# Padding 48-row products to 128 rows, and alternating the two heads of a pair, in the state-space branch of a hybrid decoder block

## The chip, the cores and the metric

The kernel runs on one core of one Trainium2 chip. The metric is the device time of one execution in microseconds. A core has a matrix engine (TensorE: PE in the profile, and PEld for its weight loads), a vector engine (DVE), a scalar engine (ACT), a general engine (POOL) and a queue engine (SP) that here only issues transfers. About 0.2% (some 2 us) is what a measurement of this kernel can tell from no change.

## The reference

One layer of a gated block over 512 tokens of width 1024, in float32: a normalisation, one wide input projection, three token mixers (a state-space scan, a top-k attention, a pooling mixer), each up-projected and gated, one output projection, a feed-forward part and a last normalisation. The change lies in the state-space scan. It has 16 heads of width 64 in 2 groups, and works on 4 chunks of 128 tokens:

```python
a_cs = jnp.cumsum(a, axis=2)
seg = a_cs[:, :, :, None] - a_cs[:, :, None, :]
lmat = jnp.exp(jnp.where(causal, seg, -jnp.inf))
cb = jnp.einsum('bclgn,bcsgn->bclsg', Cc, Bc)
y_diag = jnp.einsum('bclsg,bclsgj,bcsgjp->bclgjp', cb, lmat, x)
...
y_off = jnp.einsum('bclgn,bcgjpn,bclgj->bclgjp', Cc, prev, jnp.exp(a_cs))
return (y_diag + y_off).reshape(b, T, g, j, p).astype(out_dtype)
```

So each head needs its running sum `a_cs` spread over a 128x128 square per chunk (for `lmat`), and again over its 64 output rows (for `exp(a_cs)`).

## The kernel before

Large products are feature-major: weights are split into a high and a low part (`wh` by ACT, `wl` by DVE), and each group of 128 output features takes 8 steps of three 128x512 matmuls (`product`, L244 to L250) into a PSUM tile `mm`, `up` or `f`. These fill the matrix engine from start to end. After every step `tick()` lets a stream of small work put its next few matmuls between the big ones: the attention heads, then the scan. The matrix engine runs its instructions in the order in which the program writes them (a count of estimated costs in `_Clock` decides when a stream may step); the other engines' order is set by a scheduler. All small products take PSUM tiles named by their use.

The scan works in pairs of heads, `ssd_pair(f)` for f from 0 to 7, two pairs in progress at a time (L800 to L845). For each of the two heads:

- `seg` (L812): one matmul of the head's running sum, kept in `acsT`, against a column of `sel`, so that every one of 128 output rows holds that sum for all 512 tokens. `acsT` holds 48 rows: the sums of 16 heads in a rounded part, a second copy, and a rest part; `sel` picks a head's rows. The matmul contracts over these 48 rows.
- `L` (L813 to L818): DVE takes the minimum with `acs`, ACT makes four exponentials of 128x128, DVE multiplies by `cbt`.

Then for the pair: `ebc` (L822) spreads the sums over the pair's 128 output rows (again 48 rows contracted, 384 columns), ACT makes `E` of it. `yd` (L825 to L830) is the in-chunk product: for each head and chunk one float32 matmul with 64 output rows, head 0 to rows 0 to 63 of the tile and head 1 to rows 64 to 127. In the trace a float32 matmul is two passes, so the 8 matmuls are 16 records. `yo` (L834) is the part that comes from the state, 128 rows and 128 columns, and DVE and POOL put the parts together. `acsT` and `sel` are written long before, in the prologue and in `dt_prep` (L525 to L529).

A matmul row of the profile such as `seg<-acsT,sel 48*128 48x512` contracts over 48 rows, has 128 output rows and streams 512 columns; `128*64` has 64 output rows.

Of the kernel before, what the change touches and what calls it, by code (L numbers as in the profile page):

```python
# [8 lines left out]
F32 = mybir.dt.float32  # L9
R32 = mybir.dt.float32r  # L10
AF = mybir.ActivationFunctionType
OP = mybir.AluOpType

P = 128
T = 512
D = 1024
NT = T // P
# [43 lines left out]


class _Engine:
    """Forwards to an engine and keeps an estimate of the work queued on it."""

    def __init__(self, name, eng, clock):
        self.name, self.eng, self.clock = name, eng, clock
# [28 lines left out]
def kernel(  # L96
# [25 lines left out]
    PE, ACT = _Engine("PE", nc.tensor, clk), _Engine("ACT", nc.scalar, clk)  # L122
    DVE, POOL = _Engine("DVE", nc.vector, clk), _Engine("POOL", nc.gpsimd, clk)
# [9 lines left out]
    streams = []  # L133

    class Stream:
        """Chains of work that fill in between the steps of the big products, up to `width` of them at once."""

        def __init__(self, gens, width, urgent=False):
            self.gens, self.width, self.live, self.urgent = list(gens), width, [], urgent
# [48 lines left out]
    def nm(s):  # L188
        uid[0] += 1
        return f"{s}_{uid[0]}"  # L190

    def const(shape, name, dtype=F32):
        return cpool.tile(shape, dtype, name=name, tag=name)

    def slot(tag, name, dtype=F32, shape=(P, T)):
        return spool.tile(list(shape), dtype, name=nm(name), tag=tag, bufs=SLOTS[tag])

    def small(shape, name, bufs=2, dtype=F32):
        return tiny.tile(list(shape), dtype, name=nm(name), tag=name, bufs=bufs)
# [10 lines left out]
    def tsl(t):  # L210
        return slice(t * P, (t + 1) * P)
# [39 lines left out]

    halves = (slice(0, T // 2), slice(T // 2, T))

# [1 line left out]
    win = w_in[0]  # L255
    xf = x[0]
    ones = const([P, P], "ones")
# [23 lines left out]
    ident = const([P, P], "ident")  # L281
# [86 lines left out]
            evac(ps)  # L368
        job(lambda: split_w(src, (P, KD, P)), body)

# [1 line left out]
    def stack(src, tag, name):  # L372
        outs = []
        for a in range(2):
# [21 lines left out]
    first = [split_w(r, (P, KD, P), e) for r, e in ((raw0[:, :, tsl(0)], POOL), (raw0[:, :, tsl(1)], POOL), (raw1[:, :, tsl(0)], DVE))]  # L396
# [16 lines left out]
    expA = const([P, 16], "expA")  # L413
    SP.dma_start(expA, row_bcast(a_log, 16))

    sel = const([48, 16], "sel", R32)
    DVE.tensor_tensor(sel, ident[0:48, 0:16], ident[0:48, 32:48], op=OP.add)
    DVE.reciprocal(ratio, ratio)
    for g in range(4):
        DVE.tensor_scalar(ratio[:, g, :], ratio[:, g, :], float(2 << g), None, OP.mult)  # L420
# [63 lines left out]
    def dt_prep():  # L484
        n = NT * 16
        dv = dt.rearrange("p c h -> p (c h)")
        tc.keep_in_program_order(ACT.activation(expA, expA, AF.Exp))
        ab = small([P, n], "sp0", 1)
        DVE.scalar_tensor_tensor(ab, dv, -1.0, dv, OP.mult, OP.max)
        e = small([P, n], "sp1", 1)  # L490
        ACT.activation(e, ab, AF.Exp, scale=-1.0)
        den = ab
        DVE.tensor_scalar(den, e, 2.0, None, OP.add)
        DVE.reciprocal(den, den)
        s = e
        DVE.tensor_tensor(s, e, den, op=OP.mult)
        z = den
        DVE.tensor_tensor(z, s, s, op=OP.mult)
        q = small([P, n], "sp2", 1)
        DVE.tensor_scalar(q, z, 1.0 / 15.0, None, OP.mult)  # L500
        for c in (13.0, 11.0, 9.0, 7.0, 5.0, 3.0):
            DVE.scalar_tensor_tensor(q, q, 1.0 / c, z, OP.add, OP.mult)
        DVE.scalar_tensor_tensor(q, q, 1.0, s, OP.add, OP.mult)
        DVE.tensor_scalar(dv, dv, 0.0, None, OP.max)
        DVE.scalar_tensor_tensor(dv, q, 2.0, dv, OP.mult, OP.add)
        a = small([P, NT, 16], "sa", 1)
        DVE.scalar_tensor_tensor(a, dt, -1.0, expA[:, None, :].to_broadcast([P, NT, 16]), OP.mult, OP.mult)
        a3 = small([P, NT, 3, 16], "a3", 1)
        DVE.tensor_copy(a3, a[:, :, None, :].to_broadcast([P, NT, 3, 16]))
        av = a.rearrange("p c h -> p (c h)")  # L510
        yield
        ps = paux("acs")
        PE.matmul(ps[:, 0:n], lhsT=triu, rhs=av, start=True, stop=True)
        acv = acs.rearrange("p c h -> p (c h)")
        DVE.tensor_copy(acv, ps[:, 0:n])
        DVE.tensor_scalar(nacs.rearrange("p c h -> p (c h)"), acv, -1.0, None, OP.mult)
        yield
        ps = paux("alast")
        PE.matmul(ps[:, 0:n], lhsT=ones, rhs=av, start=True, stop=True)
        ACT.activation(dch.rearrange("p c h -> p (c h)"), ps[:, 0:n], AF.Exp)  # L520
        dec = small([P, n], "sp1", 1)
        DVE.tensor_tensor(dec, ps[:, 0:n], acv, op=OP.subtract)
        ACT.activation(decay.rearrange("p c h -> p (c h)"), dec, AF.Exp)
        yield
        ps = paux("acsT")  # L525
        for c in range(NT):
            PE.matmul(ps[0:48, tsl(c)], lhsT=a3[:, c].rearrange("p r h -> p (r h)"), rhs=triu, start=True, stop=True)
        ACT.copy(acsT, ps[0:48, :])
        DVE.tensor_tensor(acsT[32:48, :], ps[32:48, :], acsT[32:48, :], op=OP.subtract)  # L529
        yield  # L530

# [1 line left out]
    nacs = const([P, NT, 16], "nacs")  # L533
    dch = const([P, NT, 16], "dch")
    decay = const([P, NT, 16], "decay")
    acsT = const([48, T], "acsT", R32)

    bias = [None] + [slot("A", "bias") for _ in range(3)]
    picked = {0}
    Stream([kd_tokens()] + [scores(b, bias[b]) for b in range(1, NT)] + [dt_prep()]  # L540
           + [topk(b, bias[b]) for b in range(1, NT)], 1)

# [1 line left out]
    pw = slot("m", "poolw", shape=(P, 4, P))  # L544
    AQ.dma_start(pw, pool_w[0].rearrange("g c d -> c g d"))
    pwh = slot("m", "poolwh", R32, (P, 4, P))
# [43 lines left out]
        for s in range(2):  # L590
            proj_job(raw[:, :, tsl(s)], pool_evac(2 * j + s))

# [1 line left out]
    def k_evac(ps):  # L594
        kT.extend(double(ps, g, "T2", "kT") for g in range(2))

# [128 lines left out]
        for st in mixes:  # L725
            need(st)

# [1 line left out]
    xbc = [None] * 12  # L729

    def conv_evac(f):
# [12 lines left out]
            xbc[f] = hv  # L744
        return evac

# [1 line left out]
    zs = [None] * KD  # L748
    ssq = []
    ctx_g = [dict(xdt=[], hst=[None]) for _ in range(2)]  # L750
# [7 lines left out]
    def ssd_group(g):  # L758
        G = ctx_g[g]
        BT, CT = xbc[8 + g], xbc[10 + g]  # L760
        G["selp"] = slot("T2", "selp", R32, (48, 4, P))
        DVE.tensor_copy(G["selp"].rearrange("a b (c d) -> a (b c) d", d=64),
                        sel[:, 8 * g:8 * g + 8][:, :, None].to_broadcast([48, 8, 64]))
        ps = paux("btr")
        for c in range(NT):
            PE.transpose(ps[:, tsl(c)], BT[:, tsl(c)], ident)
        btok = slot("A", "btok")
        ACT.copy(btok, ps)
        G["btok"] = btok
        ps = paux("cbt")  # L770
        for c in range(NT):
            PE.matmul(ps[:, tsl(c)], lhsT=BT[:, tsl(c)], rhs=CT[:, tsl(c)], start=True, stop=True)
        cbt = slot("A", "cbt")
        DVE.tensor_tensor(cbt.rearrange("p (c t) -> p c t", c=NT), ps.rearrange("p (c t) -> p c t", c=NT),
                          triu[:, None, :].to_broadcast([P, NT, P]), op=OP.mult)
        G["cbt"] = cbt
        for c in range(NT):
            yield
            ps = paux("xtr")
            for i in range(4):  # L780
                PE.transpose(ps[:, tsl(i)], xbc[4 * g + i][:, tsl(c)], ident)
            xd = slot("A", "xdt")
            DVE.tensor_tensor(h8(xd), h8(ps), b8(dt, c, g), op=OP.mult)
            G["xdt"].append(xd)
            if c == NT - 1:
                break
            xdd = slot("T1", "xdd")
            POOL.tensor_tensor(h8(xdd), h8(xd), b8(decay, c, g), op=OP.mult)
            yield
            ps = paux("state")  # L790
            PE.matmul(ps, lhsT=btok[:, tsl(c)], rhs=xdd, start=True, stop=True)
            hn = slot("T2", "hst")
            if c == 0:
                ACT.copy(hn, ps)
            else:
                POOL.tensor_tensor(h8(hn), h8(G["hst"][c]), b8(dch, c, g), op=OP.mult)
                DVE.tensor_tensor(hn, hn, ps, op=OP.add)
            G["hst"].append(hn)

    def ssd_pair(f):  # L800
        g, pr = divmod(f, 4)
        G = ctx_g[g]
# [6 lines left out]
        for hh in range(2):  # L809
            j = 2 * f + hh  # L810
            ps = paux("seg")
            PE.matmul(ps, lhsT=sel[:, j:j + 1].to_broadcast([48, P]), rhs=acsT, start=True, stop=True)  # L812
            l = slot("T1", "L")  # L813
            DVE.tensor_tensor(l.rearrange("p (c t) -> p c t", c=NT), ps.rearrange("p (c t) -> p c t", c=NT),
                              acs[:, :, j:j + 1].to_broadcast([P, NT, P]), op=OP.min)
            for c in range(NT):
                ACT.activation(l[:, tsl(c)], l[:, tsl(c)], AF.Exp, bias=nacs[:, c, j:j + 1])
            DVE.tensor_tensor(l, l, G["cbt"], op=OP.mult)  # L818
            L.append(l)
            yield  # L820
        ps = paux("ebc")
# [1 line left out]
        E = slot("T1", "E")  # L823
        ACT.activation(E[:, P:], ps[:, P:], AF.Exp)
        yd = paux("yd")  # L825
        for hh in range(2):
            jl = 2 * pr + hh
            for c in range(NT):
                PE.matmul(yd[hh * 64:hh * 64 + 64, tsl(c)], lhsT=G["xdt"][c][:, jl * 64:jl * 64 + 64], rhs=L[hh][:, tsl(c)],
                          start=True, stop=True)  # L830
        DVE.scalar_tensor_tensor(xT, xT, c_dskip(f), yd, OP.mult, OP.add)
# [111 lines left out]
    gate_merge(0, w_up_ssd, 8, lambda k: ysh[k], lambda k: ysl[k], ssd_ready)  # L943
    flush()

# [1 line left out]
    def start_now(gen):  # L947
        st = Stream([gen], 1, urgent=True)
        at = clk.pe
# [122 lines left out]
    for j in range(NH // 2):  # L1072
# [12 lines left out]
        for s in range(2):  # L1085
            i = 2 * j + s
            pab = []
            for key, r in ((("a", i), ra), (("b", i), rb)):
# [4 lines left out]
                ps = pmm("f")  # L1093
# [18 lines left out]
    of = out[0]  # L1112
# [34 lines left out]
```

## Time and profile before

| | |
|---|---|
| median of 3 runs | 942.32 us (942.07 to 942.43) |
| the profiled execution, its span | 942.4 us |
| matrix engine busy | 920.5 us |
| DVE, ACT, POOL busy | 491.0, 359.8, 94.6 us |
| transfers | 85.42 MB, 91 GB/s |
| scan pairs on the matrix engine | first `seg` at 321.8 us, last `yd` at 417.8 us |

The page gives the span of the profiled execution and no other time of it; it lies 0.1 us from the median. "Busy" of the matrix engine is to be read with care: a record lasts longer than the step to the next one, since matmuls are pipelined. The time that a matmul takes from the engine is the distance from its start to the start of the next. A row of the timeline gives start, length, engine, line and operands, and in brackets the idle time before it and what ended it. All instructions that go through the kernel's engine wrapper carry line L90, so the operands tell them apart.

### The profile page before, as it was taken

The numbers are of one execution on the slowest core, as the hardware profiler recorded it, in microseconds if no ns is written. First come the engines' busy times: TensorE is split into PE (matmuls) and PEld (weight loads), VectorE is DVE, ScalarE is ACT, GpSimd is POOL, SyncE is SP. The second block draws the span as 40 slices with busy tenths as digits, with TensorE's granted clock in tenths as the row PEclk, the third lists the DMA queues.
The fourth block names the chain that finished last, engine by engine and source line by source line (L and its number), as shares of the span: only waits on it lengthen the run. The fifth ranks groups of instructions, "written<-read, shape, count | busy, mean of one in ns | idle before, by whom it ended". The sixth has DMA issues, their size and how long they took to land.

```text
span 942.4 us, 10998 instructions
## 1 busy us (share of the span) xinstructions
PE 920.5 (98%) x4401; PEld 755.8 (80%) x4401; DVE 491.0 (52%) x792; ACT 359.8 (38%) x618; POOL 94.6 (10%) x94
## 2 busy tenths in 40 slices
PE   6999899999999999999999999999999999999997
PEld 4887678888888777777888889888888888888885
DVE  6487999955654565668333455333333333322226
ACT  5446433355563344435323247223223223212114
POOL 2061000001111132232000013000000000000001
PEclk9999999999999999999999999999999999999999
DMA  7132112222212211134323241222222233233212
GB/s 236 46 112 84 52 45 90 87 92 89 89 47 63 94 45 57 46 100 148 121 90 125 98 135 45 90 90 90 90 90 89 90 104 119 90 97 122 94 45 89
DMA packets 70964, 85.42 MB, mean 91 GB/s; under 512 B 4025, under 2 KB 61953, under 8 KB 70914
## 3 DMA queue, kind: packets, MB, share of 16 engines
q1 hardware_dynamic: 69234, 82.38, 27.0%
q10 hardware_dynamic: 1680, 2.36, 0.7%
q8 instruction: 34, 0.56, 0.2%
q14 instruction: 16, 0.13, 0.0%
HBM read 82.63 MB, written 2.10 MB: 90 GB/s over the span
## 4 chain that ended last, share of the span: by engine, by line
PE 88%; DVE 8%; ACT 1%; issue 1%; POOL 1%; DMA 1%; SPq 0%; ACTq 0%; POOLq 0%; DVEq 0%
PE mm L90 28%; PE f L90 26%; PE acc L90 17%; PE up L90 8%; DVE work L90 2%; DVE wl L90 2%; PE yatt L90 1%; PE yd L90 1%; DVE top L90 1%; PE ptr L90 1%; PE logit L90 1%; PE yo L90 1%; PE seg L90 1%; POOL win L90 1%; DVE qT L90 1%
## 5 line engine op out<-in xcount | busy, mean ns | idle before, releaser
L90 DVE TENSOR_TENSOR wl<-raw,wh 128x1024 fp32r<-128x1024 f32 (+1 forms) x150 | 184.5, 1230 | 228.3 <-ACT wh L90 223.1
L90 ACT CAST wh<-raw 128x1024 fp32r<-128x1024 f32 (+1 forms) x152 | 152.7, 1005 | 383.1 <-PE f L90 155.7
L90 PE MATMUL mm<-xnh,wh 128*128 128x512 f32 (+1 forms) x480 | 196.3, 409 | 0.2 <-ACT xnh L90 0.2
L90 PE MATMUL mm<-xnl,wh 128*128 128x512 f32 (+1 forms) x480 | 184.6, 384 | 1.2 <-DVE xnl L90 1.2
L90 PE MATMUL mm<-xnh,wl 128*128 128x512 f32 (+1 forms) x480 | 184.8, 385 | 0.0
L90 PE MATMUL f<-hnh,wh 128*128 128x512 f32 x328 | 127.6, 389 | 0.0
L90 PE MATMUL f<-hnl,wh 128*128 128x512 f32 x328 | 127.6, 389 | 0.0
L90 PE MATMUL f<-hnh,wl 128*128 128x512 f32 x328 | 127.6, 389 | 0.0
L90 PEld LDWEIGHTS mm<-xnh,wh 128*128 128x128 f32 x480 | 92.5, 193 | 18.3 <-issue 4.8
L90 PEld LDWEIGHTS mm<-xnh,wl 128*128 128x128 f32 x480 | 91.8, 191 | 18.3 <-DVE wl L90 0.3
L90 PEld LDWEIGHTS mm<-xnl,wh 128*128 128x128 f32 x480 | 92.3, 192 | 15.8 <-DVE xnl L90 1.7
L90 PEld LDWEIGHTS f<-hnl,wh 128*128 128x128 f32 x328 | 61.6, 188 | 12.9
L90 PEld LDWEIGHTS f<-hnh,wh 128*128 128x128 f32 x328 | 61.6, 188 | 12.8
L90 PEld LDWEIGHTS f<-hnh,wl 128*128 128x128 f32 x328 | 61.6, 188 | 12.6
L90 DVE TENSOR_TENSOR silu<-silu,f 128x512 f32<-128x512 f32 x22 | 15.1, 688 | 78.5 <-PE f L90 78.5
L90 PE MATMUL acc<-wh,hidh 128*128 128x512 f32 x144 | 56.0, 389 | 0.0
L90 PE MATMUL acc<-wl,hidh 128*128 128x512 f32 x144 | 56.0, 389 | 0.0
L90 PE MATMUL acc<-wh,hidl 128*128 128x512 f32 x144 | 44.8, 389 | 0.0
L90 POOL TENSOR_TENSOR rows<-xr,fnrow 128x512 f32<-128x512 f32 x3 | 3.9, 1290 | 353.0 <-issue 347.4
L90 POOL TENSOR_TENSOR xbc<-xbc,tap 128x509 f32<-128x509 f32 x12 | 14.0, 1164 | 195.5 <-DVE xbc L90 167.9
L90 PEld LDWEIGHTS acc<-wh,hidh 128*128 128x128 f32 x144 | 27.0, 188 | 5.6
L90 PEld LDWEIGHTS acc<-wh,hidl 128*128 128x128 f32 x144 | 27.0, 188 | 5.6
(248 smaller groups left out, 1330.6 us busy)
## 6 DMA issues: line engine op xcount, KB each, us to landing
raw<-in_w_in_dram SPq DMA_DIRECT2D x26, 1024.0 KB, 5.0
raw<-in_w_ffn_in_dram SPq DMA_DIRECT2D x22, 1024.0 KB, 4.9
raw<-in_w_ffn_out_dram SPq DMA_DIRECT2D x11, 1024.0 KB, 5.0
raw<-in_w_up_ssd_dram SPq DMA_DIRECT2D x4, 1024.0 KB, 4.9
raw<-in_w_out_dram SPq DMA_DIRECT2D x4, 1024.0 KB, 5.0
xb<-in_x_dram SPq DMA_DIRECT2D x4, 512.0 KB, 4.1
raw<-in_w_in_dram SPq DMA_DIRECT2D x4, 512.0 KB, 6.0
raw<-in_w_up_pool_dram SPq DMA_DIRECT2D x2, 1024.0 KB, 5.2
```

The source lines that it names most:

```text
L90: return fn(*args, **kw)
```

## The change

`sel`, `acsT` and `selp` get 128 rows in place of 48. `sel` and `acsT` are set to zero once on POOL, and the code then writes their first 48 rows as before. The matmuls `seg` and `ebc` so contract over 128 rows, 80 of which are zero. In `yd` the loops over heads and chunks change places: the heads alternate. Some comments and docstrings are gone as well.

```diff
-    sel = const([48, 16], "sel", R32)
-    DVE.tensor_tensor(sel, ident[0:48, 0:16], ident[0:48, 32:48], op=OP.add)
+    sel = const([P, 16], "sel", R32)
+    POOL.memset(sel.bitcast(F32), 0.0)
+    DVE.tensor_tensor(sel[0:48, :], ident[0:48, 0:16], ident[0:48, 32:48], op=OP.add)
...
-        ACT.copy(acsT, ps[0:48, :])
+        ACT.copy(acsT[0:48, :], ps[0:48, :])
...
-    acsT = const([48, T], "acsT", R32)
+    acsT = const([P, T], "acsT", R32)
+    POOL.memset(acsT.bitcast(F32), 0.0)
...
-        G["selp"] = slot("T2", "selp", R32, (48, 4, P))
+        G["selp"] = slot("T2", "selp", R32, (P, 4, P))
...
-            PE.matmul(ps, lhsT=sel[:, j:j + 1].to_broadcast([48, P]), rhs=acsT, start=True, stop=True)
+            PE.matmul(ps, lhsT=sel[:, j:j + 1].to_broadcast([P, P]), rhs=acsT, start=True, stop=True)
...
-        for hh in range(2):
-            jl = 2 * pr + hh
-            for c in range(NT):
+        for c in range(NT):
+            for hh in range(2):
+                jl = 2 * pr + hh
                 PE.matmul(yd[hh * 64:hh * 64 + 64, tsl(c)], lhsT=G["xdt"][c][:, jl * 64:jl * 64 + 64], rhs=L[hh][:, tsl(c)],
```

On the matrix engine the first pair stands so before. The number behind a name is that of the buffer: `L_2828` is head 0, `L_2888` head 1, and the four `xdt` are the four chunks.

```order
L90 MATMUL ebc_2946<-acsT,selp_2631 128x384 [waits DVE_49]
L90 MATMUL yd_2950<-L_2828,xdt_2664 64x128 [waits DVE_49,Activation_49]
L90 MATMUL yd_2950<-L_2828,xdt_2706 64x128 [waits Activation_49]
L90 MATMUL yd_2950<-L_2828,xdt_2753 64x128 [waits Activation_49]
L90 MATMUL yd_2950<-L_2828,xdt_2805 64x128 [waits Activation_49]
L90 MATMUL yd_2950<-L_2888,xdt_2664 64x128 [waits DVE_49]
L90 MATMUL yd_2950<-L_2888,xdt_2706 64x128 [waits Activation_49]
L90 MATMUL yd_2950<-L_2888,xdt_2753 64x128 [waits Activation_49]
L90 MATMUL yd_2950<-L_2888,xdt_2805 64x128 [waits Activation_49]
L90 MATMUL yo_2960<-xbc_1945,hst_2693 128x128 [waits Activation_49]
```

And so now, at the same place of the matrix engine's order (two buffers more come before it, so all numbers are higher by 2: `L_2830` is head 0, `L_2890` head 1).

```order
L90 MATMUL ebc_2948<-acsT,selp_2633 128x384 [waits DVE_49]
L90 MATMUL yd_2952<-L_2830,xdt_2666 64x128 [waits DVE_49,Activation_49]
L90 MATMUL yd_2952<-L_2890,xdt_2666 64x128 [waits DVE_49]
L90 MATMUL yd_2952<-L_2830,xdt_2708 64x128
L90 MATMUL yd_2952<-L_2890,xdt_2708 64x128 [waits Activation_49]
L90 MATMUL yd_2952<-L_2830,xdt_2755 64x128
L90 MATMUL yd_2952<-L_2890,xdt_2755 64x128 [waits Activation_49]
L90 MATMUL yd_2952<-L_2830,xdt_2807 64x128
L90 MATMUL yd_2952<-L_2890,xdt_2807 64x128 [waits Activation_49]
L90 MATMUL yo_2962<-xbc_1947,hst_2695 128x128 [waits Activation_49]
```

The wait for head 1's `L` (a DVE wait) has moved from the fifth `yd` to the second. No other matmul of the program changes its place.

On POOL, in the prologue, the two fills stand between the constants and the first weight split.

```order
L90 AFFINE_SELECT negc<-negc 128x128 [waits Pool_49]
L90 AFFINE_SELECT triu<-triu 128x128 [waits Pool_49]
L90 MEMSET sel 128x16
L90 MEMSET acsT 128x512
L90 TENSOR_TENSOR wl_167<-raw_82,wh_166 128x1024 [waits DMAHW4_49,Activation_49]
```

Before, the first `wl` follows the second `AFFINE_SELECT` at once. The one other move is on ACT, in the middle of the scan, where a weight copy `wh` and a gate evacuation `gth` stood so before.

```order
L90 ACTIVATE sq_631_3202<-xbc_426_2218 128x512 [waits DVE_49,PE_49]
L90 ACTIVATE gth_634_3226<-mm_619_3137 128x512 [waits PE_49]
L90 CAST wh_638_3247<-raw_616_3131 128x512
L90 ACTIVATE L_633_3219<-L_633_3219,nacs_424 128x128 [waits DVE_49]
L90 ACTIVATE L_633_3219<-L_633_3219,nacs_424 128x128 x3
```

Now the copy comes first, and both come before the same exponentials.

```order
L90 ACTIVATE sq_631_3204<-xbc_426_2220 128x512 [waits DVE_49,PE_49]
L90 CAST wh_638_3249<-raw_616_3133 128x512 [waits PE_49]
L90 ACTIVATE gth_634_3228<-mm_619_3139 128x512 [waits PE_49]
L90 ACTIVATE L_633_3221<-L_633_3221,nacs_425 128x128 [waits DVE_49]
L90 ACTIVATE L_633_3221<-L_633_3221,nacs_425 128x128 x3
```

The orders of DVE and SP are the same as before.

## Rows read from the trace of the kernel before

**Rows 1.** The page: busy time of the matrix engine with its share and count, and the chain that ended last by engine.

```profile
PE 920.5 (98%) x4401; PEld 755.8 (80%) x4401; DVE 491.0 (52%) x792; ACT 359.8 (38%) x618; POOL 94.6 (10%) x94
PE 88%; DVE 8%; ACT 1%; issue 1%; POOL 1%; DMA 1%; SPq 0%; ACTq 0%; POOLq 0%; DVEq 0%
```

**Rows 2.** Busy time by stage, the scan and all that follows it up to the tail: length, then busy time and count of PE, PEld, DVE, ACT, POOL, then the granted clock of the matrix engine, DMA share and GB/s.

```profile
290.00:424.00 134.00, 133.62 (x661) 100.32 (x660) 79.69 (x104) 53.86 (x117) 34.36 (x29) 1.00 0.22 71
424.00:930.00 506.00, 505.28 (x2320) 421.41 (x2319) 191.67 (x219) 158.08 (x216) 20.10 (x14) 1.00 0.29 97
```

**Rows 3.** Whom the matrix engine waited for between 280 and 520 us: total, times, longest.

```profile
PE rstd L90 <- ACT rt L90: 0.7, 1, 0.7
PE yd L90 <- DVE L L90: 0.4, 1, 0.4
```

**Rows 4.** Timeline of the matrix engine around a `seg` matmul (the tenth of sixteen).

```profile
376.78 0.39 PE L90 MATMUL mm<-xnh,wl 128*128 128x512 f32 x1
377.10 0.50 PE L90 MATMUL seg<-acsT,sel 48*128 48x512 f32 x1
377.52 0.50 PE L90 MATMUL mm<-xnh,wh 128*128 128x512 f32 x1
377.86 0.40 PE L90 MATMUL mm<-xnl,wh 128*128 128x512 f32 x1
```

**Rows 5.** Timeline of the matrix engine around `mix`, another small product put between the big ones, of the pooling branch: same type and columns as `seg`, but 128 rows.

```profile
54.23 0.39 PE L90 MATMUL mm<-xnh,wl 128*128 128x512 f32 x1
54.46 0.39 PE L90 MATMUL mix<-uh,poolwh 128*128 128x512 f32 x1
54.68 0.39 PE L90 MATMUL mix<-ul,poolwh 128*128 128x512 f32 x1
54.91 0.39 PE L90 MATMUL mix<-uh,poolwl 128*128 128x512 f32 x1
```

**Rows 6.** All `seg` matmuls: count, duration in ns (least, median, most), first and last start.

```profile
L90 PE MATMUL seg<-acsT,sel x16: 491/497/499, 321.8 to 411.7; 48*128 48x512 f32 x16
```

**Rows 7.** Timeline of the matrix engine at the end of the seventh pair.

```profile
402.54 0.39 PE L90 MATMUL mm<-xnh,wl 128*128 128x512 f32 x1
402.86 0.44 PE L90 MATMUL ebc<-acsT,selp 48*128 48x384 f32 x1
403.23 1.58 PE L90 MATMUL yd<-L,xdt 128*64 128x128 f32 x16
404.74 0.94 PE L90 MATMUL yo<-xbc,hst 128*128 128x128 f32 x6
```

**Rows 8.** Timeline of the matrix engine at `acsT`, the one other place where a product with few output rows (48) follows a full one.

```profile
99.30 0.39 PE L90 MATMUL mm<-xnh,wl 128*128 128x512 f32 x1
99.62 1.07 PE L90 MATMUL acsT<-triu,a 128*48 128x128 f32 x8
```

**Rows 9.** Timeline of the matrix engine at the end of the eighth pair, where head 1's `L` came late.

```profile
415.48 1.09 PE L90 MATMUL yd<-L,xdt 128*64 128x128 f32 x8
416.94 1.09 PE L90 MATMUL yd<-L,xdt 128*64 128x128 f32 x8 [0.38 <-DVE L L90]
417.96 0.94 PE L90 MATMUL yo<-xbc,hst 128*128 128x128 f32 x6
```

**Rows 10.** The `yd` instructions alone, in stretches of 0.22 us: length, then busy time and count of records of PE, PEld and DVE, the clock, DMA. The first row is of the fourth pair, where head 0 runs alone; the others are of the second pair, at its start and in its middle.

```profile
366.83:367.05 0.22, 0.22 (x4) 0.22 (x3) 0.00 (x0) 1.00 0.00 0
...
342.43:342.65 0.22, 0.22 (x4) 0.22 (x3) 0.00 (x0) 1.00 0.00 0
342.87:343.09 0.22, 0.22 (x7) 0.22 (x5) 0.00 (x0) 1.00 0.00 0
```

**Rows 11.** Timeline around the third and fourth pair: DVE's last step of `L` for the third, the matrix engine at the third and the fourth, and DVE's last step of `L` for the fourth.

```profile
361.84 0.69 DVE L90 TENSOR_TENSOR L<-L,cbt 128x512 f32<-128x512 f32 x1
...
362.75 1.58 PE L90 MATMUL yd<-L,xdt 128*64 128x128 f32 x16
...
365.72 0.60 PE L90 MATMUL xtr<-ident,xbc 128*128 128x128 f32 x4
...
366.62 2.18 PE L90 MATMUL yd<-L,xdt 128*64 128x128 f32 x16
...
366.36 0.69 DVE L90 TENSOR_TENSOR xdt<-xtr,dt 128x512 f32<-128x512 f32 x1 [0.50 <-PE xtr L90]
366.97 0.68 DVE L90 TENSOR_TENSOR L<-L,cbt 128x512 f32<-128x512 f32 x1
```

**Rows 12.** Timeline of ACT and of DVE before the eighth pair.

```profile
412.92 1.05 ACT L90 CAST wh<-raw 128x1024 fp32r<-128x1024 f32 x1 [1.86 <-PE up L90]
...
416.21 0.68 DVE L90 TENSOR_TENSOR L<-L,cbt 128x512 f32<-128x512 f32 x1
```

**Rows 13.** Timeline of POOL in the prologue, and of ACT where `wh` and `gth` change places.

```profile
1.71 0.20 POOL L90 MEMSET triu<- 128x128 f32 x1
9.64 2.35 POOL L90 TENSOR_TENSOR wl<-raw,wh 128x1024 fp32r<-128x1024 f32 x1 [7.24 <-ACT wh L90]
...
373.24 0.61 ACT L90 CAST wh<-raw 128x512 fp32r<-128x512 f32 x1
```

**Rows 14.** The weight loads of `yd`: count, duration in ns (least, median, most), first and last start.

```profile
L90 PEld LDWEIGHTS yd<-L,xdt x128: 132/137/138, 337.6 to 417.7; 128*64 128x64 f32 x128
```

More of the change, by code (lines that the diff above doesn't have):

```diff
@@ L760, in ssd_group @@
         BT, CT = xbc[8 + g], xbc[10 + g]
-        G["selp"] = slot("T2", "selp", R32, (48, 4, P))
+        G["selp"] = slot("T2", "selp", R32, (P, 4, P))
         DVE.tensor_copy(G["selp"].rearrange("a b (c d) -> a (b c) d", d=64),
-                        sel[:, 8 * g:8 * g + 8][:, :, None].to_broadcast([48, 8, 64]))
+                        sel[:, 8 * g:8 * g + 8][:, :, None].to_broadcast([P, 8, 64]))
         ps = paux("btr")
```

## The prediction

> **What bounds the kernel now.** I read the page first, then busy time by stage, then the matrix engine's waits, then its timeline row by row inside the scan. The page shows the matrix engine busy for 98% of the span, and the chain that ended last lies on it for 88% [rows 1]. By stage it is busy for 133.62 of 134.00 us in the scan and 505.28 of 506.00 us in what follows, at a granted clock of 1.00, the 2.4 GHz level, while DVE, ACT and POOL have room (79.69, 53.86 and 34.36 us of the 134) [rows 2]. Only two waits of it show between 280 and 520 us, 0.7 and 0.4 us [rows 3]. So time taken out of the matrix engine's order in the scan comes off the end, unless what it is fed with becomes late. The question is what `seg`, `ebc` and `yd` take from the engine, and that is the distance between starts, not the length of a record.
>
> **seg, 16 times.** In the timeline, `mm` to `seg` is 377.10 - 376.78 = 0.32 us, `seg` to the next `mm` 0.42, and that `mm` to its follower 0.34: 1.08 us for three steps [rows 4]. A full product of the same type and columns put between big ones, `mix`, runs 54.23, 54.46, 54.68, 54.91: 0.68 us for three steps, and costs no more than another big matmul [rows 5]. So a 48-row product between 128-row ones is not slow in its own columns; the engine stops when it comes to it, and again when it leaves it, and each time the next weights are loaded late. With 128 rows `seg` stands where `mix` stands: 1.08 - 0.68 = 0.40 us each. All sixteen are alike (491 to 499 ns) [rows 6], so 16 x 0.40 = 6.4 us. Bounds: at worst padding gives nothing (0); at best 0.40 each, since nothing can be quicker than `mix`.
>
> **ebc, 8 times.** `mm` to `ebc` is 0.32 us and `ebc` to `yd` 0.37 [rows 7]. With 128 rows the entry becomes 0.23 as at `mix`. The exit stays a change of shape, since `yd` has 64 output rows: 384 columns at the pace of `mix` are 0.17 us, and entering a narrow product costs 0.09 more, which `acsT` shows (0.32 from a full `mm` where 0.23 is usual) [rows 8]. So 0.26 instead of 0.37, and 0.09 + 0.11 = 0.20 us each, 1.6 us for eight. Bounds: 0 and 0.20.
>
> **yd, 8 pairs.** Where head 1 was late, a head runs alone: first pass to `yo` is 417.96 - 416.94 = 1.02 us for 8 passes [rows 9]. Where both were ready, the pair takes 404.74 - 403.23 = 1.51, not twice 1.02 [rows 7]: the two heads already overlap in part. The counts show it: in 0.22 us a head alone has 4 records in progress, as does the start of the second pair, but its middle has 7, two heads at full pace each [rows 10]. The engine thus reaches ahead to head 1 when head 0 is about half through. With the heads alternating head 1 is the second matmul, so both run side by side from the start. The pair then takes 1.02 us, plus between nothing and one matmul of head 0 before head 1 starts (two passes, 0.23 to 0.26 us by a quarter of 1.02). That saves 0.49 to 0.23 us; I take 0.40, nearer to the first, because in the middle both halves overlap fully. Bounds over six such pairs: 1.4 to 2.9 us.
>
> **What is late next.** The alternation puts the wait for head 1's `L` in front of head 0's second chunk, so six passes of head 0 queue behind it, and behind them `yo` and the big products. In two pairs `L` was late already. Eighth pair: `L` ends at 416.21 + 0.68 = 416.89 and head 1 starts at 416.94 [rows 9, 12]; after that head 1's 8 passes need 1.02 us both before and now, since head 0's six run beside them. So the end of that pair is set by `L`, whose chain starts with a weight copy on ACT that the matrix engine releases at 412.92 [rows 12]; what is saved ahead of that stays, what `ebc` and `yd` save in this pair is lost. Fourth pair: `L` waits on DVE behind `xdt`, which waits for the transposes `xtr` at 365.72 [rows 11]; the same holds. Third pair: `L` was ready at 361.84 + 0.69 = 362.53, only 0.22 us before `yd`, and the engine now comes about 0.6 us sooner to it (a `seg` and an `ebc` lie between), so of its 0.40 us I keep 0.1. The other five pairs I count in full. Sum: 6.4 + 6 x 0.20 + 5 x 0.40 + 0.1 = 9.7 us.
>
> **The rest.** Two fills on POOL: a 128x128 fill takes 0.20 us, so 128x512 at four times that is 0.8 by estimate, and some 0.1 for `sel`; POOL sits idle for 7.24 us before its first split at 9.64 [rows 13], which hides them. Without that cover they would delay the first weights by 0.9 us. `selp` is as long per partition as before, and DVE's time goes by that: 0. On ACT the exchange of `wh` and `gth` delays `gth` by one copy, 0.61 us [rows 13]; both still come before the next exponentials, so nothing waits that didn't: 0, at worst 0.6. After the scan each wait hangs on the matrix engine's own products (`rstd`, 0.7 us [rows 3]) and moves with them.
>
> The profiled span, 942.4 us, is 0.1 from the median, so the sum goes on either: 942.4 - 9.7 = 932.7 us.
>
> **Rivals.**
> - *Padding does nothing, only the order does.* If the stops came from the broadcast weights or from the operand, not from the 48 rows, `seg` and `ebc` stay and `yd` gives 2.1: 940.2 us. For it: no 48-row product stands alone with plain weights. Against: `ebc` has plain weights and the same 0.32 at its entry, and `acsT`, narrow in the other direction, has it too [rows 7, 8]. Chance 0.05.
> - *The gain is eaten by feeders.* DVE is busy 60% of the scan and works in order; a `wl` or `L` late by a microsecond at each pair would take back about half, 4.8 us: 937.5 us. For it: two or three of eight `L` are already at the edge. Against: the big products show no wait for weights in 134 us [rows 3], and DVE has 54 us free there [rows 2]. Chance 0.07.
> - *Alternation exposes the weight loads: slower.* Each pass of `yd` would wait for its own load, 0.137 us [rows 14], on top of its 0.116 ((1.02 - 0.09 for the exit) / 8): 0.25 x 16 = 4.0 us for a pair instead of 1.51, so 2.5 x 6 = 15 us, and for the two late pairs 14 passes after the wait, 3.5 instead of 1.02, another 5.0. Against 7.6 us from padding that makes 12.4 us: 954.8 us. It decides the sign from 7.6 / 128 = 0.06 us a pass. Against it: in the middle of the second pair five loads and seven passes of both heads are in progress within 0.22 us [rows 10]. Chance 0.03. The Trainium skill speaks for this rival: "TensorE: Matmul & The Clock Gate", Part 3 (The mechanism), says that a weight load overlaps with matmuls in flight only where the two use other row groups, and both heads here use all 128 rows; by that rule the sum would be the 954.8 above. The trace does not agree, by the row just named.
>
> **How the numbers follow.** The forecast, all three parts at about their size, has 0.85. Its own ends: 6.4 + 1.6 + 2.9 = 10.9 us if no pair loses anything (931.5), and 6.4 + 1.4 = 7.8 if `ebc` gives nothing and `yd` its least (934.6). I let the range reach from 930.8 to 936.8, into the second rival; that leaves out the rest of it, the first and the third, about 0.15. Faster by over 0.2% (1.9 us, what a measurement here can tell from no change): the forecast, the second rival and nearly all of the first (2.1 us is close to that bound), 0.95. Slower 0.03, the same 0.02.
>
> **What would show it.** Right: every `seg` 0.23 us after its neighbour and the next two matmuls 0.23 apart; `ebc` to `yd` about 0.26; `yd` to `yo` about 1.1 us where `L` is in time; the wait for `L` before `yd` longer in the fourth and eighth pair (0.6 us or more) and perhaps new in the third; the scan shorter by 9 to 10 us, and the stage after it of the same length. Wrong: steps of 0.32 and 0.42 around a 128-row `seg` (then it isn't the rows), `yd` to `yo` above 1.5 us, or new waits for `wl` between 320 and 450 us.

## The result and the profile after

The changed kernel takes 934.04 us (median of 4 runs, 933.53 to 934.89) against 942.38 us before (942.07 to 944.32): ratio 0.9906, 95% interval 0.9894 to 0.9918, so 7.7 to 10.0 us faster. The forecast was 932.7 us, 9.7 us less, in a range from 930.8 to 936.8.

The page of the changed kernel begins like that of before, with the matrix engine's busy time and count, and has the chain by engine further down:

```profile
span 931.8 us, 11002 instructions
PE 906.9 (97%) x4401; PEld 751.2 (81%) x4401; DVE 489.2 (52%) x792; ACT 359.3 (39%) x618; POOL 96.4 (10%) x96
...
PE 85%; DVE 9%; issue 2%; ACT 2%; POOL 1%; DMA 0%; SPq 0%; POOLq 0%; ACTq 0%; DVEq 0%
```

The matrix engine has the same 4401 records and is still what bounds the kernel, as in [rows 1]; 13.6 us of its busy time are gone. The rows that answer to [rows 4], the timeline around the ninth `seg`:

```profile
365.77 0.39 PE L90 MATMUL mm<-xnh,wl 128*128 128x512 f32 x1
365.99 0.40 PE L90 MATMUL seg<-acsT,sel 128*128 128x512 f32 x1
366.23 0.39 PE L90 MATMUL up<-yah,wh 128*128 128x512 f32 x1
366.46 0.40 PE L90 MATMUL up<-yal,wh 128*128 128x512 f32 x1
```

and the group of all sixteen, against [rows 6]:

```profile
L90 PE MATMUL seg<-acsT,sel x16: 392/397/400, 320.3 to 401.5; 128*128 128x512 f32 x16
```

From the `mm` ahead of it to the second product behind it there are 366.46 - 365.77 = 0.69 us, where it was 1.08: 0.39 us each, 6.2 us for sixteen. The record of `seg` is shorter too, 397 ns instead of 497. The weight loads (PEld) show where the time was lost; the load of the tenth `seg` before, and under it that of the ninth now:

```profile
377.09 0.18 PEld L90 LDWEIGHTS seg<-acsT,sel 48*128 48x128 f32 x1 [0.35 <-issue]
```

```profile
365.77 0.19 PEld L90 LDWEIGHTS seg<-acsT,sel 128*128 128x128 f32 x1
```

With 48 rows the load starts at 377.09, just ahead of its own matmul at 377.10 [rows 4], after 0.35 us without a load. With 128 rows it starts 0.22 us ahead of its matmul (365.77 and 365.99), beside the `mm` before it. The timeline of the sixth pair answers to [rows 7]:

```profile
384.07 0.39 PE L90 MATMUL mm<-xnh,wl 128*128 128x512 f32 x1
384.29 0.33 PE L90 MATMUL ebc<-acsT,selp 128*128 128x384 f32 x1
384.56 1.09 PE L90 MATMUL yd<-L,xdt 128*64 128x128 f32 x16
385.58 0.82 PE L90 MATMUL yo<-xbc,hst 128*128 128x128 f32 x5
```

and the `yd` instructions alone, in 0.22 us of it, to [rows 10] (length, then PE and PEld):

```profile
384.82:385.04 0.22, 0.22 (x8) 0.22 (x6) 0.00 (x0) 1.00 0.00 0
```

`ebc` now comes 0.22 us after `mm` and `yd` 0.27 after `ebc`, which saves 0.20 us. `yd` to `yo` is 1.02 us, what one head alone took in [rows 9]: eight records are in progress where a head alone has four. Both heads run beside each other from their first pass.

What is given back shows in the matrix engine's waits between 280 and 520 us (total, times, longest), against [rows 3]:

```profile
PE yd L90 <- DVE L L90: 2.7, 3, 1.3
PE rstd L90 <- ACT rt L90: 0.7, 1, 0.7
```

and in the timeline of the seventh pair:

```profile
393.02 0.43 PE L90 MATMUL yd<-L,xdt 128*64 128x128 f32 x2
394.01 1.09 PE L90 MATMUL yd<-L,xdt 128*64 128x128 f32 x14 [0.56 <-DVE L L90]
395.03 0.38 PE L90 MATMUL yo<-xbc,hst 128*128 128x128 f32 x1
```

The wait for `L` has grown from 0.4 to 2.7 us. Only two passes of head 0 stand ahead of it, so 14 passes come behind. The eighth pair waits longest:

```profile
406.42 1.09 PE L90 MATMUL yd<-L,xdt 128*64 128x128 f32 x14 [1.26 <-DVE L L90]
```

From the first `yd` to `yo` the eight pairs take 1.02, 1.02, 1.46, 2.29, 1.02, 1.02, 2.01 and 2.71 us, 12.6 in all; before it was 1.51 in six pairs, 2.11 in the fourth and 2.48 in the eighth, 13.7 in all.

### The profile page after: what moved, and what is told of

It is laid out like the page before. It is cut to its first block, busy times and chain, and to the rows that moved or that the text cites. A ratio compares the mean times of both kernels' runs of the same rounds, so it can differ in the third digit from the quotient of the medians.

```text
span 931.8 us, 11002 instructions
## 1 busy us (share of the span) xinstructions
PE 906.9 (97%) x4401; PEld 751.2 (81%) x4401; DVE 489.2 (52%) x792; ACT 359.3 (39%) x618; POOL 96.4 (10%) x96
## 4 chain that ended last, share of the span: by engine, by line
PE 85%; DVE 9%; issue 2%; ACT 2%; POOL 1%; DMA 0%; SPq 0%; POOLq 0%; ACTq 0%; DVEq 0%
PE mm L90 26%; PE f L90 26%; PE acc L90 17%; PE up L90 8%; DVE work L90 2%; DVE wl L90 2%; DVE top L90 2%; PE yatt L90 1%; PE yd L90 1%; PE ptr L90 1%; PE logit L90 1%; POOL win L90 1%; PE yo L90 1%; DVE qT L90 1%; PE state L90 1%
## 5 line engine op out<-in xcount | busy, mean ns | idle before, releaser
L90 PE MATMUL mm<-xnh,wh 128*128 128x512 f32 (+1 forms) x480 | 193.9, 404 | 0.2 <-ACT xnh L90 0.2
L90 PEld LDWEIGHTS f<-hnh,wh 128*128 128x128 f32 x328 | 61.6, 188 | 12.6
L90 PEld LDWEIGHTS acc<-wl,hidh 128*128 128x128 f32 x144 | 27.0, 188 | 5.6
```

The costliest lines, as they stand in the source:

```text
L90: return fn(*args, **kw)
```

## The experiments

**Which part gives what.** My theory: a product with few rows stops the matrix engine when it comes to it and when it leaves it, and the alternation brings the two heads side by side. The first rival: only the order of heads counts. The first run keeps the padding and puts the heads back in the old order, the second keeps 48 rows and alternates.

```diff
-        for c in range(NT):
-            for hh in range(2):
-                jl = 2 * pr + hh
+        for hh in range(2):
+            jl = 2 * pr + hh
+            for c in range(NT):
```

> Padding alone, heads in the old order. My theory (the 48-row shape makes the matrix engine stop on entry and exit): every seg 0.23 us after its neighbour, ebc to yd 0.26, the six overlapped pairs stay at 1.51 us from yd to yo, the two late ones grow by 0.2 to 0.4; 942.3 - 6.4 - 1.6 + 0.6 = about 935 us. Rival (only the order of heads matters): 0.32 and 0.42 around seg stay, about 942 us.

Measured: 935.36 us (931.65 to 937.34), ratio 0.992 (0.9895 to 0.9945). The steps around a `seg` and an `ebc`:

```profile
383.90 0.39 PE L90 MATMUL mm<-xnh,wl 128*128 128x512 f32 x1
384.13 0.40 PE L90 MATMUL seg<-acsT,sel 128*128 128x512 f32 x1
384.37 0.39 PE L90 MATMUL mm<-xnh,wh 128*128 128x512 f32 x1
...
385.74 0.33 PE L90 MATMUL ebc<-acsT,selp 128*128 128x384 f32 x1
386.00 1.36 PE L90 MATMUL yd<-L,xdt 128*64 128x128 f32 x14
```

`seg` stands at 0.23 us, `ebc` to `yd` is 0.26, and five of the six overlapped pairs stay at 1.51 us. The seventh goes to 1.62, the fourth from 2.11 to 2.29 and the eighth from 2.48 to 2.71 us, these two as in the changed kernel: the padding alone is enough for their loss, since it brings the engine sooner to a late `L`. The eight pairs take 14.2 us in all. The four times lie 5.7 us apart, three of them at one mean clock (0.998); why is not shown, and the interval is wide for it.

The second run is the kernel before with the other half of that edit: its heads alternate.

```diff
-        for hh in range(2):
-            jl = 2 * pr + hh
-            for c in range(NT):
+        for c in range(NT):
+            for hh in range(2):
+                jl = 2 * pr + hh
```

> Alternation alone, 48 rows kept. My theory: pairs with both L in time go from 1.51 to 1.02 us, pairs with a late L end as before; seg keeps 0.32 and 0.42; 942.3 - 6 x 0.49 = 939.4 us, up to 940.5 if a pair that was in time becomes late. Rival (the wait moved ahead of head 0's chunks costs what the overlap gives): 942 us or more.

Measured: 940.8 us (936.15 to 941.95, 10 runs), ratio 0.9975 (0.9962 to 0.9988). The six pairs that were in time stay so and go to 1.02 us; the fourth takes 2.23 and the eighth 2.48. The timeline at the end of its sixth pair:

```profile
391.04 0.44 PE L90 MATMUL ebc<-acsT,selp 48*128 48x384 f32 x1
391.41 1.09 PE L90 MATMUL yd<-L,xdt 128*64 128x128 f32 x16
392.44 0.38 PE L90 MATMUL yo<-xbc,hst 128*128 128x128 f32 x1
```

From first `yd` to `yo` its trace saves 13.7 - 10.9 = 2.8 us. The two parts thus give 0.8% and 0.25% alone, and 0.9 to 1.0% together. They don't quite add up: on top of the padding the alternation saves only 14.2 - 12.6 = 1.6 us in the pairs, since the engine then comes sooner to an `L` that is late. The rival that only the order counts is out.

**Is it the number of rows, and which number?** The next two are the changed kernel with 64 and with 80 rows in `sel`, `acsT` and `selp` in place of 128 (here for 64):

```diff
-    sel = const([P, 16], "sel", R32)
+    sel = const([64, 16], "sel", R32)
...
-    acsT = const([P, T], "acsT", R32)
+    acsT = const([64, T], "acsT", R32)
...
-            PE.matmul(ps, lhsT=sel[:, j:j + 1].to_broadcast([P, P]), rhs=acsT, start=True, stop=True)
+            PE.matmul(ps, lhsT=sel[:, j:j + 1].to_broadcast([64, P]), rhs=acsT, start=True, stop=True)
```

> As the changed kernel, but sel, acsT and selp padded to 64 rows only. If the stop comes from using half of the array's rows (a shape of 64 rows), nothing of seg and ebc is saved: 0.32 and 0.42 around seg, time as with alternation alone, about 940 us. If it came from the operands themselves (unfilled rows, broadcast weights), 64 rows would do as well as 128: about 934 us.

> As the changed kernel, but padded to 80 rows. If the shape has steps (up to 64 rows one shape, above it the full one), 80 rows save as much as 128: seg at 0.23, about 934 us. If any product with fewer than 128 rows stops the engine, 80 rows save nothing: 0.32 and 0.42, about 940 us.

Measured: with 64 rows 940.89 us (939.23 to 941.62), ratio 0.9976 (0.9966 to 0.9985), the same as without padding. With 80 rows 934.04 us (933.77 to 934.7), ratio 0.9913 (0.9897 to 0.993), the same as with 128. The timelines around a `seg`, first with 64 rows:

```profile
389.43 0.39 PE L90 MATMUL mm<-xnh,wl 128*128 128x512 f32 x1
389.74 0.50 PE L90 MATMUL seg<-acsT,sel 64*128 64x512 f32 x1
390.17 0.50 PE L90 MATMUL mm<-xnh,wh 128*128 128x512 f32 x1
390.51 0.40 PE L90 MATMUL mm<-xnl,wh 128*128 128x512 f32 x1
```

and then with 80 rows:

```profile
382.50 0.39 PE L90 MATMUL mm<-xnh,wl 128*128 128x512 f32 x1
382.72 0.40 PE L90 MATMUL seg<-acsT,sel 80*128 80x512 f32 x1
382.96 0.40 PE L90 MATMUL mm<-xnh,wh 128*128 128x512 f32 x1
383.20 0.40 PE L90 MATMUL mm<-xnl,wh 128*128 128x512 f32 x1
```

So 1.08 us for three steps with 64 rows, 0.70 with 80. The operands are of one kind in both (filled with zeros, broadcast weights), so it isn't the operands. And it isn't that every product with fewer than 128 rows stops the engine: 48 and 64 rows stop it, 80 and 128 don't, and between 64 and 80 nothing was run.

**Is it the product or the change of shape?** In the kernel before, each 48-row `seg` is issued a second time, right behind the first and into the same tile.

```diff
             PE.matmul(ps, lhsT=sel[:, j:j + 1].to_broadcast([48, P]), rhs=acsT, start=True, stop=True)
+            nc.tensor.matmul(ps, lhsT=sel[:, j:j + 1].to_broadcast([48, P]), rhs=acsT, start=True, stop=True)
```

> The kernel before, with each seg matmul issued twice in a row into the same tile (the second repeats the first). If the engine stops at a change of shape, the second seg costs 0.21 to 0.23 us (its own columns): 942.4 + 3.6 = 946 us. If each 48-row matmul carries the stop itself, it costs 0.6 us: 952 us.

Measured: 947.82 us (946.09 to 948.06), ratio 1.0042 (1.0027 to 1.0057), 2.5 to 5.4 us slower. The timeline shows the size more sharply:

```profile
378.91 0.39 PE L90 MATMUL mm<-xnh,wl 128*128 128x512 f32 x1
379.23 0.50 PE L90 MATMUL seg<-acsT,sel 48*128 48x512 f32 x1
379.57 0.39 PE L813 MATMUL seg<-acsT,sel 48*128 48x512 f32 x1
379.88 0.50 PE L90 MATMUL mm<-xnh,wh 128*128 128x512 f32 x1
380.22 0.40 PE L90 MATMUL mm<-xnl,wh 128*128 128x512 f32 x1
```

Four steps take 380.22 - 378.91 = 1.31 us; three took 1.08. The second `seg` adds 0.23 us, as much as any full product, and 16 x 0.23 = 3.7 us is inside the interval. (Runs of equal mean clock differ by just that: 947.91 and 944.20 us at 0.997, 946.09 and 942.40 at 0.999.) The stop comes once for the change of shape, not once for each product. The record of the first product after a change of shape is long (0.50 us) on both sides, that of the second `seg` is not (0.39).

**Can the waits for L be had back?** The changed kernel gives 2.7 us to waits for `L`. In the program the place of `ebc` and `yd` follows from a count of costs; adding to it after head 1's `L` puts more big products ahead of them (the edit with 1.0 us). The changed kernel was run once more beside these.

```diff
             L.append(l)
+            if hh:
+                clk.end += 1.0
             yield
```

> The changed kernel once more, beside the next three on the same chip: 934 us, yd waits of 2.7 us in all.

> The changed kernel, with a cost of 1.0 us added to the program's own count after head 1's L, so that ebc and yd of most pairs come one to four steps of big products later. My theory (about 2 to 3 us of the gain went into waits for a late L): the yd waits fall from 2.7 to about 1 us and the time to about 932.5 us. Rival (the waits only move elsewhere, the scan is bound by the chain through DVE, ACT and POOL): 934 us, with other waits of the matrix engine in place of them.

> The same with 2.0 us. My theory: waits below 1 us, about 932 us. Rival: 934 us or more, with a longer wait at the scan's end (ssq, rstd, or the up products that need it).

Measured: 933.42 us for the changed kernel (933.07 to 935.35), ratio 0.9898 (0.9883 to 0.9913); 932.53 us with 1.0 us added (932.23 to 932.83), ratio 0.9884 (0.9868 to 0.9901); 932.11 us with 2.0 us (931.74 to 933.46), ratio 0.9883 (0.9868 to 0.9897). The two times are those that I forecast, but not for my reason. Against the changed kernel in the same set the medians are lower by 0.9 and 1.3 us, and the intervals overlap, so a gain of that size is not clear of the noise. The waits for `L` did not fall as my theory said: 3.2 us with 1.0 added, and with 2.0 added still

```profile
PE yd L90 <- DVE L L90: 2.8, 2, 1.4
```

in two pairs instead of three. For that step the rival was right, the waits had moved. What is gone in both traces is the 0.7 us wait for `rstd`; with 2.0 added the pairs also take 11.87 us instead of 12.56, with 1.0 added 12.65. The timeline of the run with 2.0 added shows where to: the fourth pair, 2.8 us behind the third, first the matrix engine, then DVE.

```profile
358.86 1.09 PE L90 MATMUL yd<-L,xdt 128*64 128x128 f32 x16
361.62 0.43 PE L90 MATMUL yd<-L,xdt 128*64 128x128 f32 x2
363.46 1.09 PE L90 MATMUL yd<-L,xdt 128*64 128x128 f32 x14 [1.41 <-DVE L L90]
...
359.98 0.69 DVE L90 TENSOR_TENSOR L<-seg,acs 128x512 f32<-128x512 f32 x1 [1.20 <-PE yd L90]
362.02 1.39 DVE L90 TENSOR_TENSOR L<-L,cbt 128x512 f32<-128x512 f32 x1 [0.23 <-ACT L L90]
```

DVE can begin the fourth pair's second `L` only when the third pair's `yd` has given back its tile (there are four of that kind). From there the chain takes 363.41 - 359.98 = 3.4 us, and the matrix engine is at the fourth pair's `yd` after 361.62 - 359.98 = 1.6. So two pairs must not follow each other so closely. The last two runs hold them apart, one with the 2.0 us and one without:

```diff
+    last_yd = [-1.0e9]
...
+        while clk.pe < last_yd[0] + 4.5:
+            yield "wait"
+        last_yd[0] = clk.pe
         ps = paux("ebc")
```

> As the run before with 2.0 us added, and also at least 4.5 us of the program's own count between the yd of one pair and the ebc of the next. My theory (the waits that are left come where two pairs follow within 3 us, since head 1 of the second gets its tile for L only when the first pair's yd is done): the two waits of 1.4 us go, the time falls by about 2.5 us to about 930 us. Rival (the scan's feeders set its pace, and a wait taken away there turns up elsewhere): 932 us.

> The changed kernel with that gap alone, without the 2.0 us. Theory: the waits that come from the tile go, those that come from a late L of the pair itself (seventh and eighth pair) stay in part; 932 us, between 931 and 933.5. Rival: 933.5 us, as the changed kernel.

Measured: with both 929.16 us (928.42 to 930.03), ratio 0.9847 (0.9833 to 0.9862); with the gap alone 930.91 us (929.63 to 931.58), ratio 0.9861 (0.9845 to 0.9878). With both, no wait of the matrix engine is left between 280 and 520 us; seven pairs take 1.02 us and the eighth 1.45, 8.6 us in all. That is 12.6 - 8.6 = 4.0 us less than in the changed kernel, with the 0.7 us for `rstd` 4.7, and the medians differ by 933.42 - 929.16 = 4.3 us (the two stand in different sets; their ratios to the kernel before, 0.9898 and 0.9847, say 4.8). With the gap alone one pair is left that waits:

```profile
PE yd L90 <- DVE L L90: 0.9, 1, 0.9
PE rstd L90 <- ACT rt L90: 0.3, 1, 0.3
```

It is the fifth pair, not the seventh or eighth as I expected, and the time is just under the 931 to 933.5 us that I gave. So the feeders' own pace is not the bound: the waits were a matter of where `ebc` and `yd` stand. The run with both is faster than both kernels of this study.

## Why the prediction was right, point by point

- **The matrix engine bounds the scan, so what is taken out of its order comes off the end.** Right. The two traces are 1.5 us apart at the first `seg` (321.8 and 320.3), 10.7 us at the end of the scan and 10.6 us at the last instruction: 9.1 us come off in the scan and next to nothing is given back behind it (0.1). The stage from there to near the end reads

```profile
412.60:920.00 507.40, 506.68 (x2327) 422.66 (x2326) 192.67 (x221) 158.25 (x217) 21.10 (x15) 1.00 0.29 97
```

  with the engine idle for 0.72 us of 507.40, as in [rows 2] for 0.72 of 506.00.
- **seg, 6.4 us.** Measured 16 x 0.39 = 6.2. The step from `mix` in [rows 5] to a padded `seg` held to 0.01 us, and the runs with 64 rows, 80 rows and a doubled `seg` show the reason given: a change of shape, paid at entry and exit, with the next weights loaded late (the two PEld rows).
- **ebc, 0.20 each.** Measured 0.20, with 0.26 to 0.27 at the exit. In the fourth and the eighth pair the time is given back to a longer wait, as forecast.
- **yd.** The mechanism was right, the size of the term was off in two ways. In pairs that are in time it saves 0.49 us, not 0.40: head 1 starts at once, so the lower end of my bracket for its start was the true one. But only four pairs are in time, where I counted five in full and part of a sixth. The third saves 0.06 (I had 0.1). The fourth and the eighth take 0.18 and 0.23 us longer, about the 0.20 of `ebc` that I had written off. **The step that failed is "the other five pairs I count in full"**: the seventh takes 2.01 us instead of 1.51, a loss of 0.50 in place of a gain of 0.40. Together yd gives 4 x 0.49 + 0.06 - 0.18 - 0.23 - 0.50 = 1.1 us where the sum had 2.1 - 0.4 = 1.7.
- **Why the seventh pair was late.** I had looked at how far `L` is ahead of `yd` in the trace of before, and not at what it is queued behind when the matrix engine comes sooner. DVE's rows before that `yd`:

```profile
389.37 0.69 DVE L90 TENSOR_TENSOR xbc<-xbc,zs 128x512 f32<-128x512 f32 x1 [1.12 <-POOL xbc L90]
390.58 0.69 DVE L90 TENSOR_TENSOR L<-seg,acs 128x512 f32<-128x512 f32 x1
392.61 1.35 DVE L90 TENSOR_TENSOR L<-L,cbt 128x512 f32<-128x512 f32 x1 [0.76 <-ACT L L90]
```

  The first step of `L` stands behind the sixth pair's tail, which waits for POOL; that chain starts at the sixth pair's `yd` and does not get shorter. And the last step took 1.35 us where it mostly takes 0.69. POOL's row beside it:

```profile
392.12 1.29 POOL L90 TENSOR_TENSOR merged<-merged,gth 128x512 f32<-128x512 f32 x1
```

  `merged` began 0.49 us before that step and ended at 393.41, `L` 0.55 us later at 393.96. The other traces bear out that one waits for the other. In all twelve there are 18 last steps of `L` that took 0.81 to 1.78 us; in each an operation of POOL had begun 0.15 to 1.05 us before it, and each ended 0.55 us after that operation. Where `merged` began 0.10 to 0.16 us after the step, as at this pair in the trace of before, the step took 0.68 to 0.71 us and `merged` 1.66 to 1.75 instead of 1.29. Head 1 started at 394.01, so by estimate 0.66 us of this pair's delay are that meeting with POOL; that POOL came first here is a matter of timing that nobody forecast. So it is a small case of the second rival, feeders that come late: it took 0.9 us of the sum, not 4.8.
- **The rivals.** Padding without effect (940.2) is refuted by the padding alone, 0.8% faster. The slower rival, exposed weight loads (954.8), is refuted by 1.02 us for a pair; the rule of the Trainium skill that I set beside it ("TensorE: Matmul & The Clock Gate", Part 3, The mechanism: loads overlap only between different row groups) did not hold for two heads that use all rows and different output halves. Nor does it hold for the big products, nearly all of 128 rows: their loads are busy for 81% of a span of which the matmuls fill 97%.
- **The rest.** The fills on POOL (0.52 and 0.11 us, less than my 0.8 and 0.1, ahead of 6.68 us of idle time), the longer `selp` and the exchange of `wh` and `gth` on ACT left no wait of their own in the trace of after; the `rstd` wait stayed at 0.7 us, as forecast.
- **The base.** I took the profiled execution as one at the median. It was not: the runs' list gives the changed kernel 933.53 us at a span of 931.8, so a time is 1.7 us more than its span, and a span of 942.4 before belongs to a run of about 944.2. The two errors, of the span and of that execution, cancelled in the median that the sum was made against: that is luck. The last section says what that execution had.

## What to carry to other kernels

In this kernel a product of 48 or 64 rows between full ones cost its columns plus a stop at each change of shape: compare the distances between starts with those around a full product, and try zero rows for such a product, since here the padding took no time of its own and 80 rows were enough. The two heads, products for different halves of the output rows, ran side by side from the start once they alternated, but then the later operand holds up both. Where the bounding engine gets faster at a place, look again at everything that feeds it there: here 4 us more were to be had by moving the products a few steps back, and a gap between the pairs was needed before that paid.

## What the runs showed of the hardware

- 64 rows cost as much as 48 (940.89 and 940.8 us) and 80 as little as 128 (934.04 us each).
- The stop is 0.39 to 0.40 us for one isolated product, about half at the entry and half at the exit, and a second product of the same shape behind it pays nothing: 0.23 us.
- The matrix engine ran passes of the two heads side by side at full pace for both: 16 passes in the time of 8, 1.02 us. Whether it is the different output halves that allow this was not tried apart.
- DVE's last step of `L` (`L<-L,cbt`) waited for an operation of POOL that had begun before it: it ended 0.55 us after that one and took up to 1.78 us instead of 0.69. The first step, which reads `seg`, did not: 0.68 us with `merged` beside it throughout.
- The granted clock fell to its lower level (1.2 GHz) for a part of the stretch from 113 to 119 us in some executions and not in others, after the engine had been idle for 1.5 to 1.9 us of the 6 us ahead of it (108 to 114 us) in each: 1.87 us in the first execution below, which kept the clock, and 1.48 in the second, which did not, so the idle time alone doesn't tell which. The rows of 114 to 120 us, of the changed kernel's first profile and, under it, of its second (length, PE, PEld, DVE, ACT and POOL, clock):

```profile
114.00:120.00 6.00, 5.90 (x30) 4.67 (x29) 5.90 (x21) 2.07 (x6) 0.00 (x0) 1.00 0.00 0
```

```profile
114.00:120.00 6.00, 5.62 (x20) 4.64 (x21) 5.26 (x18) 1.72 (x5) 0.00 (x0) 0.72 0.00 0
```

  The second execution took 935.35 us, the other three of its set 933.07 to 933.5: about 2 us. The profiled execution of the kernel before had 0.72 there too. Of the twelve traces seven show the fall, and they are the seven with a mean clock of 0.996 or 0.997 over the whole execution. Compared at equal mean clock in one set, the changed kernel is faster by 942.40 - 933.33 = 9.1 us (0.998 and 0.999) and by 944.20 - 935.35 = 8.9 us (0.997), as the scan of the traces says; the alternation alone by 2.6 and 2.9 us, where the medians of the mixed runs give 0.25%, 2.4 us. Against a change of 9 us that is no small thing, and it is why the stretches of the scan were compared here and not the spans.
